# Attention keys stored in three orders, three contiguous products per dilated unit, and four gate projections at the first sweep's end

## The chip, the cores and the metric

The kernel runs on one core of a Trainium2 chip, as one program. The metric is the time of one execution in microseconds on the device, as a median of several runs. Beside it stands one execution taken by the hardware profiler, from which all views come. The engines are named as in the profile: PE multiplies matrices (PEld are its weight loads), DVE, ACT and POOL work on vectors, SP and ACT issue transfers (DMA).

## The reference

One decoder layer on 2048 tokens of width 1024: a combined projection to q, k, v (8 heads of 64) and the gated path's u and g (512 each); attention over three dilations; a gMLP gate; an output projection; an MLP of width 4096.

```python
WINDOW_DILATIONS = ((128, 1), (512, 4), (2048, 16))
...
h = rms_norm(x, norm1_g[l])
proj = jnp.einsum('bsd,de->bse', h, w_in[l])
q, k, v, u, g = jnp.split(...)
q = rms_norm(q.reshape(B, S, ATTN_HEADS, HEAD_DIM), q_norm_g[l])
k = rms_norm(k.reshape(B, S, ATTN_HEADS, HEAD_DIM), k_norm_g[l])
a = dilated_attention(q, k, v)
m = spatial_gating(jax.nn.gelu(u), jax.nn.gelu(g), ...)
mix = jnp.concatenate([rms_norm(a, attn_out_g[l]), rms_norm(m, gmlp_out_g[l])], axis=-1)
x = x + jnp.einsum('bse,ed->bsd', mix, w_out[l])
h = rms_norm(x, norm2_g[l])
f = jnp.square(jax.nn.relu(jnp.einsum('bsd,df->bsf', h, w_ff1[l])))
x = x + jnp.einsum('bsf,fd->bsd', f, w_ff2[l])
```

For each dilation d, position t attends to t, t-d, t-2d and so on, down to t-window (128 steps back). The three branches are combined by their softmax denominators, so they can share one maximum per position and head.

## The kernel before

Numbers are kept as pairs of a high part of reduced precision (F32R) and a low rest; a product of two such pairs is three PE products (hi x hi, lo x hi, hi x lo).

**Sweep 1** (0 to 387 us of the profile) runs over 16 tiles of 128 tokens. For each, `gemm3` projects q, k and v with 24 products of 512 columns each; a tile later `behind` transposes q and k, splits them into parts and stores them head by head in DRAM: `kt_d` holds a head's keys, 64 rows of high and 64 of low parts by 2048 tokens in their natural order, `qt_d` the queries with tokens sorted by their residue modulo 16, and `v_d` the values. Sorting happens in `store_q`, once for every group G of four tiles: a copy (ACT for high, POOL for low parts) into a tile `qp`, of which there are two, and two DMAs on SP, for each of the four pairs of heads `pr`. `max1`, `max4` and `fold4` work out score maxima of dilations 1 and 4, which go to `mx_d`.

**The transition** (387 to 421 us): the gate projections of the last two tiles, 14 and 15, then `rest` with maxima that DVE paces, and the loads and maxima (`group`, product `ps_mx`) of head 0.

**Attention** (421 to about 731 us) runs over 8 heads of 20 jobs each. Jobs 0 to 7 are dilation 1, two units each; then, for each residue r of 0 to 3, two jobs of dilation 4 (two units each) and one of dilation 16 (four units). A unit is a block of 128 keys against the queries that see them: keys are the product's weights, queries its moving operand. Each unit has two products: 128 rows of keys `ks` (high and low parts) against `qh`, the high part of the queries held twice; and 65 rows, 64 of high keys `k2` and one of ones, against `q2`, the low part of the queries and a row with minus the maximum. For dilations 4 and 16 the weights are read from `ks` and `k2` with a stride of 4 or 16 elements (lines 830 and 837). Then DVE adds the mask in PSUM, ACT writes the exponential twice (`ph`, rounded, and `e`), POOL makes the rest `pl` = e - ph, and the job's products with the values, `pv`, run four jobs later (PD = 4). In jobs 5, 8, 11 and 14 (MXAT) four `ps_mx` products each find the dilation-16 maxima of the next head, with the 64 rows of the high parts. The loads of the next head (`prepare`) stand at the start of the head before, V's behind jobs 4 and 12.

In all of this SP, PE, DVE and POOL work strictly in program order (`InOrder`), so that whatever a waiting instruction of a queue is followed by, waits with it. A DMA also waits for the one that last used its semaphore, eight of which go round over the queues of SP and ACT.

**Sweep 2** (731 to 1150 us) projects u and, for all tiles but 14 and 15, the gate (`gemm_g`, 24 products of 512 columns), then does the output projection. The **MLP** (to the end) is not touched.

Of the kernel before, what the change touches and what calls it, by code (L numbers as in the profile page):

```python
# [30 lines left out]
PD, PB, EB, LOL, EVL = 4, 5, 4, 2, 1  # L31
# [4 lines left out]
MXAT = (5, 8, 11, 14)  # L36
V1AT, V4AT = 12, 4
# [3 lines left out]
GEAT = 13  # L41
# [19 lines left out]
PSB, MXB, HS0 = 4, 1, 0  # L61

# [41 lines left out]
def tile_hybrid_block(  # L104
# [35 lines left out]
    qt_d = dram.tile([H, P, S], F32, name="qt_d")  # L140
    kt_d = dram.tile([H, P, S], F32, name="kt_d")
# [4 lines left out]
    ge_d = dram.tile([2, P, GW], F32, name="ge_d")  # L146
# [169 lines left out]

    mk1 = mkp_pool.tile([P, 2, 256], F32, name="mk1")
# [16 lines left out]
    m4t, m4e = masks(4)  # L334
    m16t, m16e = masks(16)
# [4 lines left out]
    def sweep1():  # L340
        if True:
# [8 lines left out]
            wh = [zh] + [[wp.tile([P, AW], F32R, name=f"wh{c}_{k}") for k in range(KD)] for c in (1, 2)]  # L350
            wl = [zl] + [[wp.tile([P, AW], F32R, name=f"wl{c}_{k}") for k in range(KD)] for c in (1, 2)]
# [68 lines left out]
            def store_q(G):  # L420

                for pr in range(NG):
                    for part, src in ((0, f32(qhis[G])), (1, qlos[G])):
                        src = src[:, pr, :].rearrange("p (i s) -> p s i", s=16)
                        end = G == NT // 4 - 1
                        tag = "qn" if part == 0 and end else "qp"
                        queue = nc.scalar if part == 1 and end else nc.sync
                        qp = sp.tile([P, AW], F32, tag=tag, name="qp", bufs=2).rearrange("p (s i) -> p s i", s=16)
                        if part == 0:
                            nc.scalar.activation(qp, src, AF.Copy)  # L430
                        else:
                            nc.gpsimd.tensor_copy(qp, src)  # L432
                        for hh in range(2):
                            queue.dma_start(
                                qt_d[2 * pr + hh, part * HD : (part + 1) * HD, :].rearrange("d (s i) -> d s i", s=16)[
                                    :, :, G * 32 : (G + 1) * 32
                                ],
                                qp[hh * HD : (hh + 1) * HD],
                            )
# [65 lines left out]
            qhis, qlos = {}, {}  # L505
# [41 lines left out]

            last = None
            gsrc = w_in[:, 3 * AW + GW : 3 * AW + 2 * GW]
            for t in range(NT):  # L550
# [5 lines left out]
                for c in range(3):  # L556
# [53 lines left out]
    def attention(finish, xnp, xs, tpe, wu):  # L610
        with ExitStack() as st:
# [12 lines left out]
            def prepare(h):  # L624
# [31 lines left out]
                def group(r0, psm=psm, queue=sy):  # L656
# [836 lines left out]
```

## Time and profile before

| what | value |
|---|---|
| median of 3 runs | 2432.99 us (2431.91 to 2437.35) |
| the profiled execution | 2441.18 us |
| its span | 2439.5 us |
| its mean granted PE clock | 0.963 |
| PE busy | 2357.1 us (97%) |
| PE clock in the transition, 386 to 421 us | 0.58 |
| PE clock in the attention, 421 to 731 us | 0.85 |
| PE clock in the MLP, 1150 to 2439 us | 0.99 |
| DMA busy share in the transition and the attention | 0.98 and 0.64 |

The three clocks are means of the windows between the stages' bounds. A window's row gives its length, then busy time and instruction count for each engine, then the granted clock, the share of time in which the 16 DMA engines were busy, and what they moved in GB/s. A timeline's row gives start, length, engine, line, operation, output and inputs, rows and columns; in brackets stands the time that the engine sat idle before it and what ended it. Matmuls overlap, so the pace is read from start to start, not from a length.

### The profile page before, as it was taken

What the parts mean: (1) busy time and instruction counts of PE and PEld (TensorE: products, weight loads), DVE (VectorE), ACT (ScalarE), POOL (GpSimd) and SP (SyncE); (2) the same over time, 40 slices, a digit from 0 to 9 for tenths busy, and PEclk for the clock granted to TensorE, in tenths of its full rate; (3) what the DMA queues carried; (4) which work ended last, traced back from release to release, by engine and by line L of the source; (5) the groups of instructions that cost most, each with busy time, mean ns of one, the idle gap of its engine ahead of it and who ended that gap; (6) DMA issues with size and microseconds to landing.
All of it is one profiled execution on the core that took longest, in us unless ns stands there. A gap on an engine that the chain in (4) does not pass through costs nothing. (4 is left out here: it accounts for less than half of the span.)

```text
span 2439.5 us, 31701 instructions
## 1 busy us (share of the span) xinstructions
PE 2357.1 (97%) x11292; PEld 1958.9 (80%) x11292; DVE 1461.1 (60%) x2940; ACT 973.0 (40%) x1584; POOL 843.3 (35%) x657
## 2 busy tenths in 40 slices
PE   8999997999997999998989999999999999999999
PEld 6777775999996788886778887788878888888887
DVE  6556666565565665665775557655557566565542
ACT  5323222656673222223544555555543232222321
POOL 1000001555551122222566666667752001131210
PEclk9999997789898999998999999999999999999999
DMA  6435247656744433333666556654559665575652
GB/s 195 87 79 118 61 101 166 187 150 192 197 148 104 102 89 97 92 89 117 203 191 191 150 154 194 195 155 148 155 177 335 217 198 190 182 241 180 190 172 78
DMA packets 432301, 382.34 MB, mean 157 GB/s; under 512 B 89704, under 2 KB 358632, under 8 KB 427528
## 3 DMA queue, kind: packets, MB, share of 16 engines
q1 hardware_dynamic: 415408, 377.68, 53.1%
q10 hardware_dynamic: 16736, 2.65, 0.7%
q8 instruction: 89, 1.46, 0.3%
q14 instruction: 68, 0.56, 0.1%
HBM read 259.80 MB, written 120.39 MB: 156 GB/s over the span
## 5 line engine op out<-in xcount | busy, mean ns | idle before, releaser
L1292 PE MATMUL ps_f<-hop,wop 128*128 128x512 f32 x2688 | 620.1, 392 | 11.9 <-ACT c L1300 3.2
L1414 PE MATMUL ps_f<-split 128*128 128x512 f32 x2688 | 611.1, 390 | 2.8 <-ACT c L1279 2.8
L1292 PEld LDWEIGHTS ps_f<-hop,wop 128*128 128x128 f32 x2688 | 507.6, 189 | 122.7 <-ACT hop L188 4.3
L1414 PEld LDWEIGHTS ps_f<-split 128*128 128x128 f32 x2688 | 505.8, 188 | 108.2 <-ACT c L1279 3.2
L1204 POOL TENSOR_TENSOR as<-w1r 128x512 f32<-128x512 f32 x160 | 213.5, 1342 | 164.9 <-DVE wop L189 149.6
L188 ACT ACTIVATE split<-sr 128x1024 fp32r<-128x1024 f32 x112 | 118.4, 1060 | 330.5 <-PE ps_f L1414 325.6
L1204 POOL TENSOR_TENSOR c<-c 128x512 f32<-128x512 f32 x160 | 233.7, 1485 | 45.0 <-ACT c L1280 30.7
L1424 DVE TENSOR_TENSOR acc<-acc,ps_f 128x512 f32<-128x512 f32 x192 | 124.4, 682 | 206.1 <-PE ps_f L1414 205.9
L1204 POOL TENSOR_TENSOR raw<-raw 128x1024 f32<-128x1024 f32 x40 | 101.4, 2543 | 420.8 <-DMA raw<-in_w_ff_dram 388.6
L74 POOL TENSOR_TENSOR pl<-e,ph 128x512 fp32r<-128x512 f32 x144 | 175.6, 1231 | 154.8 <-ACT e L74 127.0
L189 DVE TENSOR_TENSOR wop<-as,wop 128x512 fp32r<-128x512 f32 x160 | 149.5, 935 | 91.3 <-ACT wop L188 88.9
L188 ACT ACTIVATE wop<-as 128x512 fp32r<-128x512 f32 x160 | 100.3, 629 | 214.0 <-POOL as L1204 128.0
L74 DVE TENSOR_TENSOR ps_as<-ps_as,mk 128x512 f32<-128x512 f32 (+1 forms) x160 | 105.7, 663 | 122.8 <-PE ps_as L74 112.9
L189 DVE TENSOR_TENSOR split<-sr,split 128x1024 fp32r<-128x1024 f32 x112 | 162.9, 1455 | 16.6 <-ACT split L188 12.0
L74 PE MATMUL ps_o<-ph,v 128*64 128x128 f32 (+3 forms) x816 | 154.0, 276 | 1.4 <-ACT nacc L74 1.4
L74 PE MATMUL ps_as<-qh,ks 128*128 128x256 f32 (+1 forms) x384 | 143.0, 378 | 0.0
L74 ACT ACTIVATE ph<-ps_as 128x512 fp32r<-128x512 f32 (+1 forms) x160 | 92.4, 577 | 126.8 <-DVE ps_as L74 126.6
L432 POOL COPY qp<-qlo 128x512 f32<-128x512 f32 x16 | 17.1, 1074 | 363.5 <-DVE qlo L411 155.3
L74 PE MATMUL ps_as<-q,k 65*128 65x256 f32 (+1 forms) x384 | 139.1, 370 | 0.0
L452 DVE CUSTOM_DVE_ANT_0 jk<-ps_sc,mk 128x256 f32<-128x256 f32 (+1 forms) x232 | 92.5, 399 | 53.3 <-PE ps_sc L448 47.2
L74 PEld LDWEIGHTS ps_o<-ph,v 128*65 128x65 f32 (+1 forms) x816 | 114.4, 157 | 1.6 <-ACT nacc L74 1.6
L74 PEld LDWEIGHTS ps_as<-qh,ks 128*128 128x128 f32 x384 | 108.0, 281 | 3.0
(262 smaller groups left out, 4080.8 us busy)
## 6 DMA issues: line engine op xcount, KB each, us to landing
s_d<-c SPq DMA_DIRECT2D x224, 256.0 KB, 2.2
sr<-s_d SPq DMA_DIRECT2D x112, 512.0 KB, 3.6
raw<-in_w_ff_dram SPq DMA_DIRECT2D x96, 512.0 KB, 4.8
w1r<-in_w_ff_dram SPq DMA_DIRECT2D x128, 256.0 KB, 3.2
v<-v_d SPq DMA_DIRECT2D x24, 1040.0 KB, 12.8
xt<-in_x_dram SPq DMA_DIRECT2D x32, 512.0 KB, 4.1
raw<-h_d SPq DMA_DIRECT2D x28, 512.0 KB, 5.5
v_d<-vt SPq DMA_DIRECT2D x16, 520.0 KB, 6.2
```

What stands on the lines that cost most here:

```text
L74: return self.tc.keep_in_program_order(op(*args, **kwargs))
L188: en.scalar.activation(dst_hi, raw, AF.Copy)
L189: (en.gpsimd if on_pool else en.vector).tensor_tensor(dst_lo, raw, f32(dst_hi), ALU.subtract)
L432: nc.gpsimd.tensor_copy(qp, src)
L452: order[1].tensor_tensor_reduce(jk[:, :n], ps[:, j, :n], mk, 1.0, -3e38, ALU.add, ALU.max, accum_out=m[:, col : col + 1])
L1204: nc.gpsimd.tensor_tensor(dst, a, b, op)
L1292: nc.tensor.matmul(ps[bank], a[:, k, :], b[k], start=first and k == n == 0, stop=(k == 3 and n == 2), skip_group_check=True,)
L1414: nc.tensor.matmul(ps, s[a][:, k, :], t[b][:, k % 2, :], start=k == m == 0, stop=k == NH - 1 and m == 2)
L1424: nc.vector.tensor_tensor(c, c, ps, op)
```

## The change

1. Keys are stored three times: `kt_d` as before, `k4_d` with tokens sorted by residue modulo 4, `k16_d` modulo 16. `store_g` makes 24 sorted copies for each of the first three groups, nearly all on POOL, with 48 DMAs on SP (before, 8 copies and 16 DMAs); `qp` has three buffers. Of the last group only pair 0 is stored in sweep 1; the 18 copies and 36 DMAs of pairs 1 to 3 stand in `finish`, behind head 0's first loads.
2. Dilation 4 and 16 read their weights contiguously from tiles `k4` and `k16`. A unit there has three products: 128 rows against `qh`, 65 rows against `q2` (whose row 64 is zero), and 66 rows of a constant `sel` that picks out row 65 of `q2`, minus the maximum. `ps_mx` runs over 128 rows, with `qh` and `k16`. `k1` and `k4` have one buffer: `k4` of a head is loaded at the head's start, `k1` of the next behind job 9.
3. The value projections of tiles 14 and 15 move behind the last q and k, and the gate projections of tiles 12 and 13, with their x loaded and transposed again, join those of 14 and 15 there; sweep 2 has two gate projections fewer. The masks of dilations 4 and 16 are made at the transition.

```diff
@@ constants
-PD, PB, EB, LOL, EVL = 4, 5, 4, 2, 1
+PD, PB, EB, LOL, EVL = 4, 5, 3, 1, 1
...
-MXAT = (5, 8, 11, 14)
-V1AT, V4AT = 12, 4
+MXAT = (6, 9, 11, 13)
+V1AT, V4AT, K1AT = 12, 4, 9
...
-GEAT = 13
+PRE = (14, 15, 12, 13)
...
+QPB = 3
@@ DRAM
-    qt_d = dram.tile([H, P, S], F32, name="qt_d")
-    kt_d = dram.tile([H, P, S], F32, name="kt_d")
+    qt_d, kt_d, k4_d, k16_d = (dram.tile([H, P, S], F32, name=f"{n}_d") for n in ("qt", "kt", "k4", "k16"))
@@ sweep 1, the stores of a group of four tiles
-            def store_q(G):
-                for pr in range(NG):
-                    for part, src in ((0, f32(qhis[G])), (1, qlos[G])):
...
-                        qp = sp.tile([P, AW], F32, tag=tag, name="qp", bufs=2).rearrange("p (s i) -> p s i", s=16)
-                        if part == 0:
-                            nc.scalar.activation(qp, src, AF.Copy)
-                        else:
-                            nc.gpsimd.tensor_copy(qp, src)
...
+            def store_by(dst, m, G, pr, part, src, sync):
+                end = G == NT // 4 - 1
+                n = 512 // m
+                tag = "qn" if part == 0 and end else "qp"
+                qp = sp.tile([P, AW], F32, tag=tag, name="qp", bufs=2 if tag == "qn" else QPB).rearrange("p (s i) -> p s i", s=m)
+                src = f32(src).rearrange("p (i s) -> p s i", s=m)
+                if end and part == 0 and pr == 0:
+                    nc.scalar.activation(qp, src, AF.Copy)
+                else:
+                    nc.gpsimd.tensor_copy(qp, src)
+                if sync is None:
+                    sync = nc.scalar if part == 1 and end else nc.sync
+                for hh in range(2):
+                    rows = dst[2 * pr + hh, part * HD : (part + 1) * HD, :].rearrange("d (s i) -> d s i", s=m)
+                    sync.dma_start(rows[:, :, G * n : (G + 1) * n], qp[hh * HD : (hh + 1) * HD])
+
+            def store_g(G, todo, sync=None):
+                cols = slice((G % 2) * 512, (G % 2 + 1) * 512)
+                for pr, part in todo:
+                    k, q = (klos[G][:, pr, :], qlos[G][:, pr, :]) if part else (kring[:, pr, cols], qhis[G][:, pr, :])
+                    store_by(qt_d, 16, G, pr, part, q, sync)
+                    store_by(k16_d, 16, G, pr, part, k, sync)
+                    store_by(k4_d, 4, G, pr, part, k, sync)
...
                     if tg == 3:
-                        store_q(G)
+                        store_g(G, [(pr, part) for part in (1, 0) for pr in range(NG)] if G < NT // 4 - 1 else ((0, 0), (0, 1)))
@@ sweep 1, its end
                 for c in range(3):
+                    if c == 2 and t >= NT - 2:
+                        behind(t - 1, *last, c)
+                        continue
...
             for t in (NT - 2, NT - 1):
                 _, xh, xl, r = xs[t]
                 ps = psm.tile([P, AW], F32, tag="mm", name="ps_mm")
+                gemm3(ps, [(xh[:, k, :], xl[:, k, :], wh[2][k], wl[2][k]) for k in range(KD)])
+                keep_v(t, ps, r)
+            for n, t in enumerate(PRE):
+                if t < NT - 2:
+                    xs[t] = load_x_t(xp, pst, t, newton=True)
...
-            def finish(pe, dve):
+            def finish(pe, dve, sy):
                 order[:] = pe, dve
+                store_g(G, [(pr, part) for pr in range(1, NG) for part in (0, 1)], sy)
@@ attention, the loads of a head
-                sy.dma_start(f32(qh[0:HD, :]), qt_d[h, 0:HD, :])
-                sy.dma_start(f32(ks[0:HD, :]), kt_d[h, 0:HD, :])
-                sy.dma_start(f32(ks[HD:P, :]), kt_d[h, HD:P, :])
+                sy.dma_start(f32(k16), k16_d[h])
+                for half in range(2):
+                    sy.dma_start(f32(qh[half * HD : (half + 1) * HD, :]), qt_d[h, 0:HD, :])
                 sy.dma_start(f32(q2[0:HD, :]), qt_d[h, HD:P, :])
-                sy.dma_start(f32(qh[HD:P, :]), qt_d[h, 0:HD, :])
-                sy.dma_start(f32(k2[0:HD, :]), kt_d[h, 0:HD, :])
...
+                def load_k(m):
+                    k = first.pop(m, None)
+                    if k is None:
+                        k = (tp if m == 1 else sp).tile([P, S], F32R, tag=f"k{m}", name=f"k{m}", bufs=1)
+                    T.append(k)
+                    sy.dma_start(f32(k), (kt_d if m == 1 else k4_d)[h])
+                    if m == 1:
+                        sy.dma_start(f32(k2[0:HD, :]), kt_d[h, 0:HD, :])
@@ attention, the products
-                        pe.matmul(ps[:, j, :], qh[0:HD, s * P : (s + 1) * P], ks[0:HD, s::16], start=True, stop=True)
+                        pe.matmul(ps[:, j, :], qh[:, s * P : (s + 1) * P], k16[:, s * P : (s + 1) * P], start=True, stop=True)
...
-                for ks, k2, qh, q2, w in units:
-                    pe.matmul(ps[:, n : n + w], ks, qh, start=True, stop=False)
-                    pe.matmul(ps[:, n : n + w], k2, q2, start=False, stop=True)
+                for pairs, w in units:
+                    for j, (k, q) in enumerate(pairs):
+                        pe.matmul(ps[:, n : n + w], k, q, start=j == 0, stop=j == len(pairs) - 1)
...
+                def three(k, q, q2):
+                    return (k, q), (k[0 : HD + 1], q2[0 : HD + 1]), (sel[0 : HD + 2], q2)
...
-                            kk, qq = slice(s0, s0 + 509, 4), slice(32 * cb, 32 * cb + n)
-                            units.append((ks[:, kk], k2[:, kk], qv[:, r, :, qq], q2v[:, r, :, qq], 4 * n))
+                            kk, qq = slice(512 * r + cb * P, 512 * r + (cb + 1) * P), slice(32 * cb, 32 * cb + n)
+                            units.append((three(k4[:, kk], qv[:, r, :, qq], q2v[:, r, :, qq]), 4 * n))
...
-                        kk, qq = slice(s, None, 16), slice(s * P, (s + 1) * P)
-                        units.append((ks[:, kk], k2[:, kk], qh[:, qq], q2[:, qq], P))
+                        kk = slice(s * P, (s + 1) * P)
+                        units.append((three(k16[:, kk], qh[:, kk], q2[:, kk]), P))
@@ attention, the loop over heads
             for h in range(H):
+                load_k(4)
                 jobs = head_jobs(h, T)
...
+                    if h + 1 < H and i == K1AT:
+                        load_k(1)
@@ sweep 2
-                if t >= NT - 2:
+                if t in PRE:
                     return None
```

On PE, in head 0, a group of maxima products for head 1 and a job of dilation 4 with a whole and a half unit, before (`ks` and `k` are the two key tiles, `qh` and `q` the queries, `ps_o` the first value product behind):

```order
L74 MATMUL ps_mx<-ks,qh 128x128 x4
L74 MATMUL ps_as<-qh,ks 128x256
L74 MATMUL ps_as<-q_3869,k_3870 128x256
L74 MATMUL ps_as<-qh,ks 128x128
L74 MATMUL ps_as<-q_3869,k_3870 128x128
L74 MATMUL ps_o<-ph,v_4137 65x4x64
```

The same place on PE in the changed kernel, where k_4401 is head 1's `k16` and k_4398 head 0's `k4`:

```order
L75 MATMUL ps_mx<-k_4401,qh 128x128 x4
L75 MATMUL ps_as<-qh,k_4398 128x256
L75 MATMUL ps_as<-q_4142,k_4398 128x256
L75 MATMUL ps_as<-q_4142,sel 128x256
L75 MATMUL ps_as<-qh,k_4398 128x128
L75 MATMUL ps_as<-q_4142,k_4398 128x128
L75 MATMUL ps_as<-q_4142,sel 128x128
L75 MATMUL ps_o<-ph,v_4479 65x4x64
```

Two products of a unit have become three. On SP, from head 0's first loads to those of head 1, before (k_3870 is `k2`, v_3881 is V of dilation 1):

```order
L74 DMA k_3870<-kt_d 64x2048
L74 DMA v_3881<-v_d 128x16x130
L74 DMA qh<-qt_d 64x2048
L74 DMA ks<-kt_d 64x2048 x2
L74 DMA q_4058<-qt_d 64x2048
L74 DMA qh<-qt_d 64x2048
```

And in the changed kernel, with what each waits for, the start of the stores that now stand between them (k_d with runs of 32 is `k16_d`, with runs of 128 `k4_d`):

```order
L75 DMA v_4108<-v_d 128x16x130 [waits DMAHW7_49,PE_49]
L75 DMA qt_d<-qp 1024x1x32 [waits DMAHW0_49,Pool_49]
L75 DMA qt_d<-qp 1024x1x32 [waits DMAHW1_49]
L75 DMA k_d<-qp 1024x1x32 [waits DMAHW2_49,Pool_49]
L75 DMA k_d<-qp 1024x1x32 [waits DMAHW4_49]
L75 DMA k_d<-qp 256x1x128 [waits DMAHW5_49,Pool_49]
L75 DMA k_d<-qp 256x1x128 [waits DMAHW6_49]
L75 DMA qt_d<-qp 1024x1x32 [waits DMAHW7_49]
L75 DMA qt_d<-qp 1024x1x32 [waits DMAHW0_49]
L75 DMA k_d<-qp 1024x1x32 [waits DMAHW1_49]
L75 DMA k_d<-qp 1024x1x32 [waits DMAHW2_49]
L75 DMA k_d<-qp 256x1x128 [waits DMAHW3_49]
```

The last row shown is the eleventh of the 36 stores; the semaphore DMAHW3 that it waits for was last used by ACT's store of the maxima behind `rest(range(4, 8))`. The load of `k4` for head 0 and the loads of head 1 follow the 36th. On POOL, the last rows ahead of head 0's first `pl` in the changed kernel:

```order
L429 COPY qp<-kring 128x512
L429 COPY qp<-qhi 128x512
L429 COPY qp<-kring 128x512
L429 COPY qp<-qlo 128x512
L429 COPY qp<-klo 128x512 x2
L429 COPY qp<-kring 128x512
L659 MEMSET q_4403 2x2048
L75 TENSOR_TENSOR pl<-e,ph 128x512 x7
```

Before, only two small copies and a memset stood there; now the copies of the moved stores do, each of which needs a `qp` buffer that an earlier store has left. On PE, the end of the first sweep in the changed kernel (the last gate projection's last products, then `rest`, `ps_mx` and head 0):

```order
L226 MATMUL ps_mm<-zl_3618,xh 128x512
L227 MATMUL ps_mm<-zh_3614,xl 128x512
L479 MATMUL ps_tr<-ident,m_4023 8x128
L501 MATMUL ps_tr<-ident,m_4055 8x128 x4
L75 MATMUL ps_sc<-kring,qhi 128x256 x8
L75 MATMUL ps_tr<-ident,m_4055 8x128 x4
L75 MATMUL ps_mx<-k_4140,qh 128x128 x16
L75 MATMUL ps_mx<-ident,m_4150 16x128
L75 MATMUL ps_sc<-kring,qhi 128x256 x16
L75 MATMUL ps_tr<-ident,m_4055 8x128 x4
L75 MATMUL ps_as<-qh,k_4107 128x256
```

The maxima's `ps_sc` products of the last tile that stood behind the gates now stand ahead of them, and four gate projections instead of two precede `rest`.

More of the change, by code (lines that the diff above doesn't have):

```diff
@@ L349, in sweep1 @@
             zh, zl = wg_tiles()
-            wh = [zh] + [[wp.tile([P, AW], F32R, name=f"wh{c}_{k}") for k in range(KD)] for c in (1, 2)]
-            wl = [zl] + [[wp.tile([P, AW], F32R, name=f"wl{c}_{k}") for k in range(KD)] for c in (1, 2)]
+            wh, wl = {0: zh}, {0: zl}
+            for w, c in ((wh, 2), (wh, 1), (wl, 1), (wl, 2)):
+                w[c] = [wp.tile([P, AW], F32R, name=f"w{'h' if w is wh else 'l'}{c}_{k}") for k in range(KD)]
             vts = []
@@ L514, in behind @@
                         qhis[G] = sp.tile([P, NG, 512], F32R, tag="qhi", name="qhi")
-                        qlos[G] = sp.tile([P, NG, 512], F32, tag="qlo", name="qlo", bufs=1)
-                    los["k"] = sp.tile([P, NG, P], F32R, tag="klo", name="klo")
+                        qlos[G] = sp.tile([P, NG, 512], F32R, tag="qlo", name="qlo", bufs=1)
+                        klos[G] = sp.tile([P, NG, 512], F32R, tag="klo", name="klo", bufs=1)
                     pos = t % 8
@@ L546, in late4, with keep_v @@
                     store_m(G, range(H))
+            def keep_v(t, ps, r):
+                vt = vts[t % 2]
+                split_sb(vt[:, :, 0:HD], vt[:, :, HD + 2 : VW], ps.rearrange("p (h d) -> p h d", d=HD), r)
+                nc.sync.dma_start(v_d[:, t * P : (t + 1) * P, :].rearrange("h t c -> t h c"), f32(vt))
             last = None
@@ L641, in prepare @@
                 V = {}
-                T = [ks, qh, k2, q2, V]
+                T = [qh, q2, k16, V]
+                def load_k(m):
[6 more added lines that the diff above has]
+                        sy.dma_start(f32(k2[0:HD, :]), kt_d[h, 0:HD, :])
                 def load_v(part):
                     if part == 1:
-                        V[1] = v_tile(tp, "v1")
+                        V[1] = first.pop("v", None)
+                        if V[1] is None:
+                            V[1] = v_tile(tp, "v1")
                         sy.dma_start(f32(V[1]), v_d[h].rearrange("(b i) c -> i b c", i=P))
@@ L664, in row @@
                         dve.tensor_scalar(nm, ps[:16, 0, :], -1.0, None, ALU.mult)
-                        queue.dma_start(f32(q2[HD : HD + 1, :]), f32(nm))
+                        queue.dma_start(f32(q2[HD + 1 : HD + 2, :]), f32(nm))
                     def turn():
@@ L681, in group @@
                     return reduce
-                return T, group, load_v
+                return T, group, load_v, load_k
             later, splits = [], []
@@ L692, in due @@
                     f()
-            T, group, load_v = prepare(0)
+            T, group, load_v, load_k = prepare(0)
+            load_k(1)
             load_v(1)
             act.activation(root, ones_c, AF.Exp)
-            more = finish(pe, dve)
+            more = finish(pe, dve, sy)
             if X0S is None:
@@ L754, in head_jobs @@
             def head_jobs(h, T):
-                ks, qh, k2, q2, V = T
+                qh, q2, k16, V, ks, k4 = T
                 nacc = sp.tile([HD + 1, S], F32, tag="nacc", name="nacc")
@@ L896, in attention @@
                 if h + 1 < H:
-                    T, group, load_v = prepare(h + 1)
+                    T, group, load_v, load_k = prepare(h + 1)
                 for i, (units, msk, fin) in enumerate(jobs):
```

85 lines of the change are left out of this document (38 added, 47 removed).

## The prediction

> **What bounds the kernel now.** I read the chain of work that ended last, then the table of windows head by head, then timelines of single products. The chain is TensorE (PE) almost alone, and the page's largest lines on it belong to the MLP, which the change doesn't touch. What can be won has to come from the attention, cut here at the starts of its eight heads.
>
> ```profile
> PE 35%; DMA 1%; POOL 1%; issue 1%; ACT 0%; DVE 0%; SPq 0%; DVEq 0%; POOLq 0%; ACTq 0%
> core 0: us, PE busy (x) PEld busy (x) DVE busy (x) ACT busy (x) POOL busy (x), PEclk, DMA share, GB/s
> 421.00:461.00 40.00, 39.99 (x235) 38.86 (x236) 20.02 (x58) 22.69 (x43) 21.61 (x18) 0.69 0.56 145
> 461.00:505.00 44.00, 44.00 (x292) 43.08 (x291) 24.08 (x64) 25.92 (x48) 22.70 (x19) 0.73 0.68 178
> 505.00:540.00 35.00, 35.00 (x258) 34.19 (x257) 21.33 (x60) 22.92 (x42) 20.93 (x18) 0.95 0.66 177
> 540.00:574.00 34.00, 34.00 (x253) 33.19 (x252) 21.14 (x59) 22.55 (x43) 21.77 (x18) 1.00 0.74 199
> 574.00:611.00 37.00, 37.00 (x269) 36.19 (x268) 21.96 (x62) 23.61 (x44) 21.77 (x18) 0.91 0.71 188
> 611.00:655.00 44.00, 44.00 (x292) 43.08 (x292) 24.10 (x64) 25.98 (x48) 22.52 (x19) 0.73 0.68 177
> 655.00:690.00 35.00, 35.00 (x259) 34.19 (x258) 21.34 (x60) 22.76 (x42) 21.08 (x18) 0.95 0.79 233
> 690.00:727.00 37.00, 34.63 (x258) 33.98 (x256) 26.02 (x36) 28.80 (x55) 23.17 (x18) 0.91 0.33 118
> sum 306.00, PE 303.63 PEld 296.74 DVE 179.97 ACT 195.23 POOL 175.56; mean PE 37.95 PEld 37.09 DVE 22.50 ACT 24.40 POOL 21.94
> ```
>
> PE has no idle time in heads 0 to 6, and PEld, the weight loads, is nearly as full; no other engine is near its limit. The same program takes 34 us where the granted clock is 1.00 and 44 where it is 0.73. So two things are lost: clock, and time in which a product waits for its weights.
>
> ```profile
> 471.00:485.00 14.00, 14.00 (x81) 13.49 (x80) 6.53 (x24) 8.64 (x16) 7.31 (x7) 0.83 1.02 307
> 485.00:502.00 17.00, 17.00 (x94) 16.77 (x94) 7.14 (x19) 8.08 (x15) 7.10 (x6) 0.50 0.15 35
> 502.00:521.00 19.00, 19.00 (x151) 18.46 (x149) 12.00 (x31) 13.04 (x25) 11.38 (x10) 0.95 1.02 261
> ```
>
> Inside a head the clock falls in the part with strided keys (here 0.50) and comes back with the next head's dilation-1 jobs.
>
> **Term 1, the weights.** Start to start at full clock, in head 3:
>
> ```profile
> 542.19 0.29 PE L74 MATMUL ps_as<-q,k 65*128 65x256 f32 x1
> 542.32 0.29 PE L74 MATMUL ps_as<-qh,ks 128*128 128x256 f32 x1
> 542.44 0.29 PE L74 MATMUL ps_as<-q,k 65*128 65x256 f32 x1
> 542.56 0.23 PE L74 MATMUL ps_o<-ph,v 128*65 128x128 f32 x1
> ...
> 553.05 0.39 PE L74 MATMUL ps_as<-qh,ks 128*128 128x128 f32 x1
> 553.27 0.38 PE L74 MATMUL ps_as<-q,k 65*128 65x128 f32 x1
> 553.49 0.39 PE L74 MATMUL ps_as<-qh,ks 128*128 128x128 f32 x1
> ...
> 555.51 0.40 PE L74 MATMUL ps_as<-qh,ks 128*128 128x256 f32 x1
> 555.75 0.40 PE L74 MATMUL ps_as<-q,k 65*128 65x256 f32 x1
> 555.98 0.40 PE L74 MATMUL ps_as<-qh,ks 128*128 128x256 f32 x1
> 556.22 0.39 PE L74 MATMUL ps_as<-q,k 65*128 65x256 f32 x1
> 556.45 0.28 PE L74 MATMUL ps_o<-ph,v 128*65 128x256 f32 x1
> ...
> 557.08 0.69 PE L74 MATMUL ps_mx<-ks,qh 64*128 64x128 f32 x4
> 557.70 0.51 PE L74 MATMUL ps_as<-qh,ks 128*128 128x256 f32 x1
> ```
>
> With contiguous keys a 256-column product takes (542.56 - 542.19)/3 = 0.122 us, with keys at stride 4 (556.45 - 555.51)/4 = 0.235, with keys at stride 16 and 128 columns 0.22; an mx product takes 0.62/4 = 0.155. For 128 columns on contiguous weights the nearest row is the transposes of the second sweep, 8 in 0.79 us, 0.10 each:
>
> ```profile
> 1096.94 1.03 PE L276 MATMUL ps_tr<-ident,xt 128*128 128x128 f32 x8
> 1097.73 0.48 PE L225 MATMUL ps_mm<-woh,mh 128*128 128x512 f32 x1
> ```
>
> I take 0.11, between 0.10 and 0.122. The change gives each such unit a third product, so a full dilation-4 unit goes from 2 x 0.235 = 0.47 to 3 x 0.122 = 0.366 (12 per head: 1.25 us), the four half ones and the 16 of dilation 16 from 0.44 to 0.33 (20 x 0.11 = 2.2), the 16 mx products from 0.155 to 0.11 (0.7). Together 4.2 us a head, **33 us** in eight; the dilation-1 jobs stay. A head at full clock would be 34.0 - 4.2 = 29.8 us.
>
> ```profile
> L74 PEld LDWEIGHTS ps_as<-qh,ks x384: 186/312/339, 421.1 to 725.0; 128*128 128x128 f32 x192
> ```
>
> The loads' minimum of 186 ns is that of contiguous keys, the median of 312 that of strided ones. [...]
>
> The change also lets mx run on 128 rows instead of 64. I give that no price of its own: here no row has both counts with the same stride. [...]
>
> **Term 2, the clock.** The eight windows hold 306 us, 8 x 34 = 272, and head 7 has 2.4 us of idle PE: 306 - 272 - 2.4 = **32 us** go to the clock. In the strided part a 256-column product streams 0.12 us of its 0.235, in the new form all of its 0.122, so the array is fuller just where the clock falls. I take all 32, with 0 as the other bound, since in head 3 the same program kept its clock and the old part is thus near the edge. [...]
>
> **Term 3, the transfers.** Per head the loads of keys and queries grow from 3.15 to 5.24 MB (three key tensors of 1.05, the low half's 0.52, qh twice 0.52, q2 0.52). In head 3 DMA was busy 0.74 x 34 = 25.2 us with 199 GB/s, 6.8 MB. The 2.1 MB more take 6.8 us at 307 GB/s and 8.0 at 261, both rows above with a full DMA. So 32 to 33.2 us of transfers stand against 29.8 of PE: DMA becomes the bound of heads 1 to 6. Also k4 has one buffer and can be fetched only after the old head's last dilation-4 job; behind it k16 and qh of the next head must land before job 6, some 7 us into the head, where mx reads them: 3.1 MB need 10 to 12 us. I take 32.5 a head: 6 x 2.7 = **16 us** are given back. Bounds: 30 (nothing) and 36.
>
> **Term 4, head 0.** The order shows the last group's stores for pairs 1 to 3 (18 copies on POOL, 36 DMAs) between V1's load and k4's on SP, and on POOL ahead of the first pl. One of the stores (k4_d, the eleventh) waits, on a shared DMA semaphore, for the maxima's store behind rest(4..8), which is the last thing before head 0; 26 are left then.
>
> ```profile
> 103.38 23.27 SPq L434 DMA_DIRECT2D qt_d<-qp  x16
> ...
> L432 POOL COPY qp<-qlo 128x512 f32<-128x512 f32 x16 | 17.1, 1074 | 363.5 <-DVE qlo L411 155.3
> ...
> L74 POOL TENSOR_TENSOR pl<-e,ph 128x512 fp32r<-128x512 f32 x144 | 175.6, 1231 | 154.8 <-ACT e L74 127.0
> ```
>
> Sixteen such stores took 23.3 us with two buffers, 1.45 each; at that pace 26 need 38 us. Now five buffers serve them, two for the high and three for the low parts, and by bytes alone 3.4 MB at 261 GB/s would be 13. I take 24, between the two. The last copy stands some 6 us ahead of the last store, and the first pl behind it. PE runs ahead only by five jobs of scores, 20 products or 2.4 us, and then waits for pl: about 17 us. Then k4 (1 MB), k16 and qh of head 1 follow on SP, 9 us or more after the stores, while mx of head 1 stands at job 6: another 11. I take **28 us**, bounds 10 and 40.
>
> **Term 5, the end of sweep 1.**
>
> ```profile
> 385.95 0.39 PE L225 MATMUL ps_mm<-zh,xh 128*128 128x512 f32 x1
> 386.17 0.39 PE L226 MATMUL ps_mm<-zl,xh 128*128 128x512 f32 x1
> 386.40 0.39 PE L227 MATMUL ps_mm<-zh,xl 128*128 128x512 f32 x1
> ...
> 404.35 3.64 PE L74 MATMUL ps_mx<-ks,qh 64*128 64x128 f32 x16 [2.75 <-DMA ks<-kt_d]
> ```
>
> Two gate gemms of 24 products at 0.226 us, 10.9 us, leave sweep 2, where PE has no gaps, and come in here with 16 more transposes (1.6 us) and two waits for x's split. What they can hide is DVE's pace in rest() and the 2.75 us wait for keys, yet DVE's maxima are queued behind the same PE order. I take **+1 us** net (-6 to +6). The reordered value products cost nothing: only their place changes.
>
> **Term 6, sweep 1.** Each of the first three groups has 24 copies on POOL (26 us at 1.07) and 48 DMAs on SP instead of 16. x is loaded some tiles ahead, so SP's burst of about 45 us hides there; but the next tile's qlo and klo have one buffer and wait for the low copies, 12 pairs in about 23 us against a tile of 23.3. I take **+3 us** (0 to 12).
>
> **The sum.** -33 - 32 + 16 + 28 + 1 + 3 = -17 us, against the profiled execution's 2441.2 us (span 2439.5 and 1.7 outside it): 2424, or 0.9930 of it. The median of the runs is 2433.0, 0.3% under the profiled one; the same share of it gives **2416 us**.
>
> **The rivals**, at the median's level.
> - *Nothing collides*: the stores run at the rate of their bytes, k16 lands in time, DMA hides. Head 0 loses 10 instead of 28, heads 1 to 6 take 30: 2416 - 18 - 15 = 2383. For it: DMA stands at 0.74 in head 3 and much faster loads occur (307 GB/s). Against: the order on SP and POOL. 0.20.
> - *The clock stays as it is*: term 2 is lost, but a head is then 29.8 + 4 = 33.8 us by PE, which hides the 32.5 of the transfers, and term 3 goes with it: 2416 + 32 - 16 = 2432. For it: stalls on DMA thin out the array again. Against: the denser strided part, and head 3. 0.14.
> - *Slower, the transfers set every head*: at 235 GB/s, between the 199 of head 3's mean and the 261 above, a head's 8.9 MB take 38 us instead of 32.5, and the late mx stalls PE so that the clock falls too: 6 x 5.5 + 8 = 41, 2457. It decides from 35.4 us a head on, 17/6 = 2.9 over the value taken, where the sum is 0. 0.18.
> - *It doesn't do what it says*: strided weights gone but the loads' time not, since weight loads from contiguous 65 and 66 rows are no shorter. Terms 1 and 2 fall, and 256 products more at 0.235 us add 60: 2541. The 186 ns of the dilation-1 keys speak against it. 0.02.
>
> **How the numbers follow.** The forecast has 0.46. A measurement of this kernel tells about 0.2%, 5 us, from no change. Faster than 2428: the forecast mostly (0.40), the first rival (0.20) and some of the second (0.05): 0.65. Within: 0.15. Slower: 0.20. The range reaches from the first rival, a little further down for bounds of terms 5 and 6, to the middle between the second and third: 2375 to 2445.
>
> **What would show it.** In the new profile: weight loads of ps_as in strided jobs near 187 ns (term 1); granted clock of 0.95 or more in heads 2 to 6 (term 2); heads 1 to 6 at 30 to 36 us with PE idle before ps_mx or behind k4, k16, qh (term 3); in head 0 an idle PE of some 17 us before the first ps_o, released by POOL, with qp copies just ahead on POOL (term 4); head 0's first product at 430 to 435 us instead of 421 and sweep 2 shorter by 11 (term 5). Wrong it would be, above all, if SP's queue does not stand still at the eleventh store, or if the heads go at PE's 29.8 us.

## The result, and the profile after

The changed kernel takes 2518.61 us, median of four runs (2510.84 to 2528.23), beside 2432.45 us of the kernel before (2427.13 to 2437.35). The ratio is 1.0357, with the interval 1.0312 to 1.0401: **slower**, where 2416 us was forecast, and above the whole range. The profiled execution took 2528.23 us (span 2526.5, mean clock 0.955), 87.0 us more span than before. A ratio below leaves out executions more than 1.5% above the fastest of their kernel; there are two of them, both of sort_sb64. Cut at the ends of the stages, in us, with the forecast's terms put into the same stages:

| stage, up to | before: ends, takes | after: ends, takes | difference | forecast |
|---|---|---|---|---|
| sweep 1 and transition: first `ps_as` | 421.1, 421.1 | 471.1, 471.1 | +50.0 | +14.9 (terms 5 and 6, and the two gates) |
| attention: last `nacc` | 731.0, 309.9 | 813.0, 341.9 | +32.0 | -21 (terms 1 to 4) |
| sweep 2: first `ps_f` | 1179.6, 448.6 | 1267.5, 454.5 | +5.9 | -10.9 (the two gates) |
| MLP: end of the span | 2439.5, 1259.9 | 2526.5, 1259.0 | -0.9 | 0 |
| sum | | | +87.0 | -17 |

The chain of waits still reads as one engine. That it says PE is what hides the loss: it follows what released what, and a product on a halved clock is PE too.

```profile
PE 34%; DMA 1%; DVE 1%; POOL 1%; issue 1%; ACT 0%; SPq 0%; POOLq 0%; DVEq 0%
```

First the weights, of the tile `ps_as` (duration in ns as minimum, median and maximum, then first and last start):

```profile
L75 PEld LDWEIGHTS ps_as<-qh,k x384: 186/190/336, 471.1 to 806.6; 128*128 128x128 f32 x192
```

The median load fell from 312 to 190 ns, as term 1 said. The windows of the whole attention, of before and then of after, show PE's busy time:

```profile
421.00:731.00 310.00, 307.15 (x2127) 299.88 (x2128) 182.87 (x459) 199.11 (x368) 177.47 (x147) 0.85 0.64 176
```
```profile
471.00:813.00 342.00, 276.31 (x2383) 271.33 (x2384) 176.68 (x461) 198.42 (x368) 192.13 (x161) 0.86 0.77 219
```

PE is busy 276.3 us instead of 307.2, 30.8 less, with 256 products more. But it now stands idle 342.0 - 276.3 = 65.7 us, where it was 2.9, and the clock stayed at 0.86 (0.85): half clock covers 95.9 us of it, where it covered 93.2. PE's waits in that stretch (sum, times, longest) name the idle time:

```profile
PE ps_mx L75 <- DMA qh<-qt_d: 35.6, 7, 9.9
PE ps_o L75 <- POOL pl L75: 22.5, 3, 21.4
PE ps_mx L75 <- DVE m L75: 4.7, 14, 0.5
```

So 58 of the 66 us are two things: `ps_mx` waits for `qh`, once in each of heads 0 to 6, and head 0 waits for its first `pl`. The windows of heads 1 to 6 show the first:

```profile
530.00:571.00 41.00, 34.78 (x304) 34.26 (x303) 21.74 (x66) 24.13 (x46) 22.06 (x19) 0.88 0.73 220
571.00:609.00 38.00, 33.84 (x300) 33.33 (x298) 21.28 (x61) 23.61 (x45) 21.61 (x19) 0.91 0.85 236
609.00:647.00 38.00, 34.44 (x302) 33.75 (x300) 21.92 (x67) 24.34 (x46) 22.12 (x19) 0.91 0.82 241
647.00:685.00 38.00, 33.53 (x298) 33.01 (x298) 21.17 (x59) 23.52 (x45) 21.62 (x18) 0.91 0.80 237
685.00:725.00 40.00, 33.49 (x296) 33.12 (x297) 20.85 (x57) 23.21 (x44) 21.19 (x19) 0.87 0.82 226
725.00:765.00 40.00, 34.77 (x312) 34.11 (x310) 22.64 (x70) 25.14 (x49) 22.97 (x20) 0.91 0.83 226
```

A head takes 38 to 41 us, 38.8 by the spacing of its maxima's step `nm` on DVE (38.1 before), not 32.5. DMA is at 0.73 to 0.85 and not full, so its mass doesn't set the pace. In the third of these heads the timeline has

```profile
628.53 1.12 PE L75 MATMUL ps_mx<-k,qh 128*128 128x128 f32 x4 [2.62 <-DMA qh<-qt_d]
```

and the windows around it

```profile
620.00:624.00 4.00, 4.00 (x42) 4.00 (x41) 3.40 (x5) 3.67 (x8) 3.58 (x3) 1.00 1.04 297
624.00:628.00 4.00, 1.91 (x19) 1.65 (x17) 2.30 (x3) 2.94 (x6) 4.00 (x5) 1.00 1.02 223
628.00:632.00 4.00, 3.47 (x19) 3.47 (x20) 1.40 (x9) 0.80 (x3) 1.15 (x1) 0.55 0.99 257
632.00:636.00 4.00, 4.00 (x26) 4.00 (x26) 1.09 (x2) 2.10 (x4) 1.82 (x2) 0.60 1.04 431
636.00:640.00 4.00, 3.98 (x38) 3.84 (x36) 2.06 (x10) 2.88 (x5) 0.47 (x1) 1.00 1.07 363
```

The wait ends, and then the clock is halved for 6.8 us: 19 to 26 products in a window instead of 42. Over heads 1 to 6 the waits are 25.7 us and the halved stretches behind them 47.8, of which half, 24, is lost; (25.7 + 24)/6 = 8.3 us a head, and 38.8 - 8.3 = 30.5 is what is left.

Head 0 and the stages before it, from PE's timeline:

```profile
408.72 0.79 PE L225 MATMUL ps_mm<-zh,xh 128*128 128x512 f32 x1 [7.32 <-ACT zh L191]
...
428.06 0.79 PE L225 MATMUL ps_mm<-zh,xh 128*128 128x512 f32 x1 [5.71 <-ACT xh L195]
...
442.84 0.80 PE L225 MATMUL ps_mm<-zh,xh 128*128 128x512 f32 x1 [5.44 <-ACT xh L195]
...
496.95 0.48 PE L75 MATMUL ps_o<-pl,v 128*65 128x256 f32 x1 [21.45 <-POOL pl L75]
...
512.43 1.12 PE L75 MATMUL ps_mx<-k,qh 128*128 128x128 f32 x4 [9.95 <-DMA qh<-qt_d]
```

The late gates wait three times, 18.5 us together, and run their first products 0.43 us apart instead of 0.23. POOL's and SP's timelines at head 0's stall:

```profile
492.62 1.07 POOL L429 COPY qp<-kring 128x512 f32<-128x512 f32 x1 [0.59 <-DMA qt_d<-qp]
493.75 1.80 POOL L659 MEMSET q<- 2x2048 f32 x1
```
```profile
464.90 0.38 SPq L75 DMA_DIRECT2D v<-v_d  x1
465.37 3.27 SPq L75 DMA_DIRECT2D qt_d<-qp  x2
...
496.37 2.83 SPq L75 DMA_DIRECT2D k_d<-qp  x4
499.31 1.05 SPq L75 DMA_DIRECT2D k<-k_d  x2
```

All 36 stores stand from 465.37 to 499.2, 0.94 us each; the first `pl` comes behind the last copy and a memset, and k4 and `qh` for the next `ps_mx` behind the last store.

### The profile page after: what moved, and what is told of

Read it like the earlier page. It is cut to its first block, busy times and chain, and to the rows that moved or that the text cites. A ratio compares the mean times of both kernels' runs of the same rounds, so it can differ in the third digit from the quotient of the medians.

```text
span 2526.5 us, 32588 instructions
## 1 busy us (share of the span) xinstructions
PE 2352.1 (93%) x11564; PEld 1946.0 (77%) x11564; DVE 1471.4 (58%) x2954; ACT 966.7 (38%) x1583; POOL 926.7 (37%) x736
## 5 line engine op out<-in xcount | busy, mean ns | idle before, releaser
L1245 POOL TENSOR_TENSOR c<-c 128x512 f32<-128x512 f32 x160 | 233.9, 1487 | 44.6 <-ACT c L1321 30.4
L189 DVE TENSOR_TENSOR split<-sr,split 128x1024 fp32r<-128x1024 f32 x112 | 156.6, 1399 | 18.1 <-ACT split L188 13.3
L75 DVE TENSOR_TENSOR ps_as<-ps_as,mks 128x512 f32<-128x512 f32 (+1 forms) x128 | 83.2, 653 | 114.2 <-PE ps_as L75 70.2
L75 PE MATMUL ps_o<-ph,v 128*64 128x128 f32 (+3 forms) x816 | 144.6, 264 | 1.9 <-ACT nacc L75 1.9
L75 PE MATMUL ps_o<-pl,v 128*65 128x128 f32 (+1 forms) x408 | 102.8, 263 | 23.5 <-POOL pl L75 22.5
L225 PE MATMUL ps_mm<-zh,xh 128*128 128x512 f32 x232 | 97.9, 423 | 19.9 <-ACT xh L195 12.6
L75 PE MATMUL ps_as<-qh,k 128*128 128x256 f32 (+1 forms) x384 | 114.9, 304 | 0.0
L75 PE MATMUL ps_as<-q,k 65*128 65x128 f32 (+3 forms) x384 | 112.5, 300 | 0.0
```

The lines of the kernel that those rows point to most:

```text
L75: return self.tc.keep_in_program_order(op(*args, **kwargs))
L189: (en.gpsimd if on_pool else en.vector).tensor_tensor(dst_lo, raw, f32(dst_hi), ALU.subtract)
L225: en.tensor.matmul(ps, ah, bh, start=(i == 0), stop=False)
L1245: nc.gpsimd.tensor_tensor(dst, a, b, op)
```

## The experiments

Times are medians, each ratio is to the kernel before on the same chip in the same minutes (2433.3 to 2436.7 us), with its 95% interval. "Attention" is the time from the first `ps_as` to the last `nacc` in the profiled execution.

### The waits in the heads

**mx_late**: the changed kernel, the next head's maxima later.

```diff
-MXAT = (6, 9, 11, 13)
+MXAT = (8, 10, 12, 14)
```

> The changed kernel with the four groups of ps_mx behind jobs 8, 10, 12 and 14 instead of 6, 9, 11 and 13. Theory W, in heads 1 to 6 PE waits at the first group for k16 and qh of the next head (2.6 us in head 2) and then runs 4 to 7 us at half clock: without that wait the heads fall from 38.5 to 34 us or less, the time by 20 to 35 us to about 2490. Rival B, the transfers' mass sets the head: PE waits elsewhere instead (k4, V, the next head's k1), heads stay at 37 to 39 us and the time within 8 us of 2518.

2500.07 us, 1.0271 (1.0229 to 1.0313); attention 312.5 instead of 341.9. Four windows of 40 us in heads 2 to 5, then two of PE's waits:

```profile
551.00:591.00 40.00, 39.19 (x382) 38.82 (x380) 28.61 (x70) 32.05 (x61) 30.61 (x26) 1.00 0.98 275
591.00:631.00 40.00, 38.23 (x365) 37.73 (x365) 26.04 (x81) 28.23 (x54) 25.02 (x21) 1.00 1.02 298
631.00:671.00 40.00, 39.26 (x382) 38.88 (x381) 27.14 (x83) 29.71 (x56) 27.54 (x23) 1.00 1.03 280
671.00:711.00 40.00, 39.45 (x386) 38.86 (x385) 27.89 (x71) 29.57 (x56) 26.87 (x23) 1.00 0.97 283
```
```profile
PE ps_o L75 <- POOL pl L75: 19.5, 1, 19.5
...
PE ps_mx L75 <- DMA qh<-qt_d: 8.9, 4, 7.1
```

With the wait gone the clock stays at 1.00 and a head takes 32.0 us, close to the 32.5 of the forecast. The place of the four groups, not the mass of the transfers, which is unchanged, made 38.8 of it. That the transfers now set the pace is not shown: DMA is full, but PE is busy 156.1 of these 160 us, 31.2 a head, and waits for transfers some 0.5 us a head.

**mx_late64**: the same with the maxima over 64 rows, as before the change.

```diff
-pe.matmul(ps[:, j, :], qh[:, s * P : (s + 1) * P], k16[:, s * P : (s + 1) * P], start=True, stop=True)
+pe.matmul(ps[:, j, :], qh[0:HD, s * P : (s + 1) * P], k16[0:HD, s * P : (s + 1) * P], start=True, stop=True)
```

> mx_late (the changed kernel, groups behind jobs 8, 10, 12 and 14) with ps_mx on 64 rows, contiguous. In mx_late heads 2 to 5 ran 160 us at a clock of 1.00. Theory R: falls at half clock come back in the dilated jobs of heads 2 to 6, 10 to 30 us in all, the time 2510 or more. Theory D: with contiguous keys and three products the array is dense enough, clock 1.00 and 2500 within 8 us.

2491.66 us, 1.0230 (1.0201 to 1.0258); clock 1.00 for 198 us on end, and 0.962 as the mean of the profiled execution, beside 0.959 in mx_late. The 64 rows of `ps_mx` did not pull the clock down here, as theory D had it.

**m128, m128_late, mx8_before**: in the kernel before, `ps_mx` on 128 rows; that with the later places; the later places alone.

```diff
-pe.matmul(ps[:, j, :], qh[0:HD, s * P : (s + 1) * P], ks[0:HD, s::16], start=True, stop=True)
+pe.matmul(ps[:, j, :], qh[:, s * P : (s + 1) * P], ks[:, s::16], start=True, stop=True)
-MXAT = (5, 8, 11, 14)
+MXAT = (8, 10, 12, 14)
```

> The kernel before with one line changed: its maxima products ps_mx run over 128 rows (high and low parts of the keys, still at stride 16) instead of 64. Theory R, the clock falls because products on 64 rows count for less in what the clock follows: granted clock of the attention up from 0.85 to 0.95 or more, heads near 34 us, the time 20 to 32 us below before (2400 to 2413). Theory D, the clock follows only how densely columns stream: 64 or 128 rows make no difference, heads stay at 34 to 44 us and the time within 6 us of before (2427 to 2439).

> The kernel before with ps_mx over 128 rows and its groups behind jobs 8, 10, 12 and 14 instead of 5, 8, 11 and 14, so that the second half of qh has landed. Theory R, 64-row products let the clock fall: the waits of m128 on qh (38 us in all) are gone, no fall of 10 to 20 us at half clock is left in heads 1 to 6, heads near 34 us, the time 20 to 30 us below before (2407 to 2417). Theory D, only the density of the columns counts: the falls of before return, the time within 6 us of before.

> The control for m128_late: the kernel before with the groups behind jobs 8, 10, 12 and 14, on 64 rows as before. Theory R: falls at half clock as before, some 30 us lost, the time within 8 us of before. Theory P, that the place of the groups and not their rows keeps the clock: as fast as m128_late.

2474.98 us, 1.0160 (1.0125 to 1.0196); 2465.18, 1.0115 (1.0088 to 1.0141); 2454.11, 1.0073 (1.0047 to 1.0099). What was expected of m128 failed: PE's waits in it show a cause that no theory had,

```profile
PE ps_mx L74 <- DMA qh<-qt_d: 38.3, 5, 9.3
```

for the kernel before loads the second half of `qh` behind the keys and `q2`, and 128 rows need it (in m128_late the same wait is still 24.9 us). So neither m128 kernel tells anything of rows. mx8_before, expected within 8 us of before, is 18 us slower: half clock covers 105 us of its attention instead of 93. Why the old places keep more of the clock was not settled.

**q64 and q128** take that wait away: in the kernel before the second half of `qh` is loaded at once behind the first, and the groups stand at jobs 10, 12, 13 and 14; q128 has m128's edit as well.

```diff
-MXAT = (5, 8, 11, 14)
+MXAT = (10, 12, 13, 14)
 sy.dma_start(f32(qh[0:HD, :]), qt_d[h, 0:HD, :])
+sy.dma_start(f32(qh[HD:P, :]), qt_d[h, 0:HD, :])
...
-sy.dma_start(f32(qh[HD:P, :]), qt_d[h, 0:HD, :])
```

> The kernel before with the second half of qh loaded right behind the first and the groups of ps_mx behind jobs 10, 12, 13 and 14, still on 64 rows. Control for q128. Theories D and R alike: falls at half clock in the strided jobs as before, 20 to 35 us lost in all; the time 2435 to 2460.

> q64 with ps_mx on 128 rows. Theory R, 64-row products bring the clock down: no falls of 10 us or more in heads 1 to 6, attention at 280 to 290 us, 20 to 30 us faster than q64. Theory D, spacing alone counts: the same falls and the same time as q64 within 8 us.

2472.69 us, 1.0145 (1.0125 to 1.0166), and 2471.04, 1.0142 (1.0117 to 1.0166): alike, but both above the 2435 to 2460 expected, as these places cost still more clock (157 us at half clock in q64's attention, 138 in q128's). A window of q64, then of q128:

```profile
460.00:500.00 40.00, 37.41 (x250) 35.91 (x250) 19.43 (x55) 22.18 (x42) 20.66 (x17) 0.76 0.66 173
```
```profile
460.00:500.00 40.00, 37.14 (x255) 36.65 (x253) 20.55 (x58) 22.80 (x44) 20.42 (x18) 0.80 0.65 173
```

Rows made no difference to the time in the kernel with strided weights either. Running `ps_mx` over 128 rows, a part of the change, brings nothing that these runs can see.

### The stores

**late_undone**: the changed kernel without its third part (values and gates of the last tiles where they were).

```diff
-PRE = (14, 15, 12, 13)
+PRE = (14, 15)
...
-                    if c == 2 and t >= NT - 2:
-                        behind(t - 1, *last, c)
-                        continue
...
-            for t in (NT - 2, NT - 1):
...
-                keep_v(t, ps, r)
```

> The changed kernel with its third part undone: value products of tiles 14 and 15 in their old place, gates of tiles 12 and 13 again in sweep 2. Theory Q, the late products cost by their waits at the first sweep's end (7.3, 5.7 and 5.4 us of idle PE ahead of them, each followed by some 4 us at half clock) and their 11 us come out nowhere in sweep 2: head 0's first product moves from 471 to about 435 us, sweep 2 stays at 450 us, the time falls by 30 to 40 us to 2480 to 2490. Rival S, the waits are those of the stores and of rest() and only move to other instructions: the first product comes 11 us earlier, sweep 2 grows by 11, and the time stays within 10 us of 2518.

2523.66 us, 1.0362 (1.0318 to 1.0406), as slow as the change. The first `ps_as` comes 10.6 us earlier (460.5) and sweep 2 takes 448.9 us again, but the attention takes 352.0, 10 more. PE's waits, from the transition on:

```profile
PE ps_mx L75 <- DMA qh<-qt_d: 51.1, 8, 15.3
PE ps_o L75 <- POOL pl L75: 21.2, 3, 20.2
```

The longest wait for `qh` is that of head 0's maxima in the transition. The late products had covered it.

**stores_back**: the changed kernel with all stores of the last group in sweep 1.

```diff
-... if G < NT // 4 - 1 else ((0, 0), (0, 1)))
+... if G < NT // 4 - 1 else [(pr, part) for pr in range(NG) for part in (0, 1)])
...
-                store_g(G, [(pr, part) for pr in range(1, NG) for part in (0, 1)], sy)
```

> The changed kernel with all four pairs' sorted stores of the last group in the first sweep, none behind head 0's loads. Theory Q, the 31 us of idle PE in head 0 (21.4 before the first value product, 10.0 before ps_mx) are those of the moved stores: they vanish, head 0's first product comes some 10 us later because its loads stand behind the stores, and the time falls by 15 to 25 us to about 2498. Rival S, the same 24 us of stores delay head 0's loads by as much as they delayed its first value product: the time stays within 6 us of 2518.

2525.60 us, 1.0366 (1.0329 to 1.0403). Head 0's stall is gone (attention 311.6), but another stands ahead of the gates, from 422 to 456 us, and the first `ps_as` comes at 496.9. Among PE's waits is

```profile
PE ps_mm L225 <- ACT xh L195: 37.9, 2, 34.1
```

as ACT, which splits x for the gates, has DMAs of the stores ahead of that in its queue.

**late_stores_mx**: stores_back, late_undone and mx_late in one.

> The changed kernel with late groups (as mx_late), without the late value and gate products (as late_undone) and with all stores in sweep 1 (as stores_back). Each was tried alone: -18, +5 and +7 us. Theory C, they hide each other, since the stores' 24 us delay whatever stands behind them until nothing waits: head 0 without a stall (-31), sweep 2 at 449 us (-4), the first product near 465 us: the time 2455 to 2470. Rival, the stores hold up ACT's queue as in stores_back (34 us ahead of the gates): first product at 490 us, the time 2480 to 2500.

2481.38 us, 1.0186 (1.0157 to 1.0216); attention only 279.5, but the first `ps_as` at 489.2, behind

```profile
PE ps_mx L75 <- DMA qh<-qt_d: 45.2, 7, 37.8
```

Here head 0's maxima wait for the whole of the stores. The attention behind them gains 30.4 us over the kernel before, of the 49 that terms 1 to 3 promised together.

**twice_tail**: mx_late with the 36 late stores made twice (the second time the same data).

```diff
                 store_g(G, [(pr, part) for pr in range(1, NG) for part in (0, 1)], sy)
+                store_g(G, [(pr, part) for pr in range(1, NG) for part in (0, 1)], sy)
```

> mx_late with the last group's 36 sorted stores of pairs 1 to 3 made twice. Theory Q, these stores stand on the path of head 0: at 0.9 to 1.4 us each the second set adds 30 to 50 us, all of it as idle PE in head 0 ahead of the first value product (19.5 us in mx_late), and the time is 2530 to 2550. Rival, head 0 waits for something else (the maxima's store, the loads' own rate): less than 10 us more, 2500 to 2510.

2538.93 us, 1.0425 (1.0385 to 1.0465), 39 us above mx_late. The wait for `pl` grows from 19.5 us to

```profile
PE ps_o L75 <- POOL pl L75: 52.0, 3, 51.0
```

31.5 us for 36 more stores, 0.88 each. So the chain of copies and stores sets the stall, and nothing hides what is added to it.

### Sorted keys without the stores

**sort_sb**: sweep 1, the transition and sweep 2 as before; the attention of the change, but `k4` and `k16` are sorted in SBUF, out of the natural keys `k1`, by four copies each on DVE (on POOL for head 0's `k16`). Dilation 1 has three products as well.

```diff
-MXAT = (5, 8, 11, 14)
+MXAT = (8, 10, 12, 14)
+K4AT, K16AT = (0, 1, 2, 3), (4, 5, 6, 7)
...
+                def turn_k(eng, dst, m, j):
+                    w = m // 4
+                    d = dst.rearrange("p (s i) -> p s i", s=m)[:, j * w : (j + 1) * w]
+                    eng.tensor_copy(d, k1.rearrange("p (i s) -> p s i", s=m)[:, j * w : (j + 1) * w])
...
+                    if i in K4AT:
+                        turn_now(dve, k4, 4, K4AT.index(i))
+                    if h + 1 < H and i in K16AT:
+                        turn_k(dve, T[2], 16, K16AT.index(i))
```

> The first sweep, its end and sweep 2 as in the kernel before; the attention of the changed kernel, but k4 and k16 are made in SBUF from the natural keys by DVE (POOL for head 0), eight copies of 512 columns a head in jobs 0 to 7, instead of being stored and loaded in three orders. k2 is dropped, dilation 1 too has three products (16 more a head, 1.9 us at 0.122). Groups of ps_mx behind jobs 8, 10, 12, 14. Theory Q, the loss of the change lies in the sorted stores and not in the products: first product near 423 us, heads 31 to 34 us at a clock of 1.00, attention near 260 us instead of 310, the time 2380 to 2400. Rival V, DVE, busy 20 of 34 us a head and nearly full in dilation 1, takes the copies' 4 us badly: heads at 36 us or more, the time 2420 or more.

2421.03 us, median of ten runs, 0.9948 (0.9923 to 0.9973): it beats both kernels, by 0.5% over the one before, but by much less than theory Q expected; the time is that of rival V. First `ps_as` at 423.7, attention 287.7 instead of 309.9, half clock in 20 us of it, 10 of them right at its start. Two windows of a head each, and the copies:

```profile
495.00:530.00 35.00, 33.52 (x321) 33.15 (x320) 29.10 (x70) 24.03 (x46) 22.70 (x18) 1.00 0.64 188
530.00:565.00 35.00, 34.22 (x325) 33.60 (x323) 28.67 (x71) 24.47 (x46) 24.56 (x19) 1.00 0.64 187
```
```profile
L75 DVE CAST k<-k x60: 580/1130/1708, 426.0 to 677.2; 128x512 fp32r<-128x512 f32 x60
```

A head is 35 us at full clock, with 1.5 us of idle PE: the copies, 1.13 us each (the 4 us for eight in rival V were an estimate that no run shows), push DVE from 21 to 29 us a head, and short waits come with it. They are not all of what lies between 35 us and the 31.7 that 29.8 and 1.9 for the added products would give: PE itself is busy 33.5.

**sort_sb2** (the copies of `k16` in jobs 7 to 10, the groups in 11 to 14) and **sort_sb64** (`ps_mx` on 64 rows, the edit of mx_late64):

```diff
-MXAT = (8, 10, 12, 14)
-K4AT, K16AT = (0, 1, 2, 3), (4, 5, 6, 7)
+MXAT = (11, 12, 13, 14)
+K4AT, K16AT = (0, 1, 2, 3), (7, 8, 9, 10)
```

> sort_sb with the copies of k16 in jobs 7 to 10 and the groups of ps_mx behind jobs 11 to 14, that is outside of the dilation-1 jobs. Rival V: 5 to 15 us faster than sort_sb. Theory Q: within 6 us of it, or slower if the next head waits for its maximum's row.

> sort_sb with ps_mx on the 64 rows of the high parts, which need the first half of qh alone. Theory D, the clock goes by how densely the columns stream and not by rows: the clock stays at 1.00 in heads 1 to 6, the 7.3 us wait for qh ahead of head 0's ps_mx shrinks, and the time is 0 to 10 us below sort_sb (2411 to 2421), below both kernels of the case. Theory R, rows count: falls at half clock of 7 to 20 us a head come back in the dilated jobs, 2440 or more.

sort_sb2: 2488.42 us, 1.0231 (1.0201 to 1.0261), attention 352.6; PE waits 18.9 us for DVE's maxima, and 17 to 24 us of every head are at half clock. sort_sb64: 2431.27 us, the median of all twelve runs, and 0.9962 (0.9941 to 0.9984), with executions from 2414.61 us at a mean clock of 0.982 to 2460.25 at 0.959; its profiled one (2447.62) has two falls of 27.3 us each. Whether its rows or chance made these was not settled.

## Why the prediction was wrong

The span grew by 87 us where the forecast had it shrink by 17. Of these 104 us, 53 are in the attention, 35 ahead of it and 17 in sweep 2 (the MLP gave 1 back).

*Term 1, the weights, -33*: right in kind, and too large. Loads take 190 ns, and PE is busy 30.8 us less, though part of that is half clock that fell on idle time in head 0. At full clock PE is busy 31.2 us a head in mx_late, not 29.8, against 34.0 before: 2.8 a head instead of 4.2, an estimated 22 us in eight heads.

*Term 2, the clock, -32*: the step that failed first. The argument was that denser products keep the clock. They did where the heads had little to wait for (mx_late: 1.00 through heads 2 to 5; sort_sb: half clock in 20 us of 288). But the prediction itself put a stall into each head, and in its sum gave the stall no effect on the clock. Half clock went from 93.2 to 95.9 us, and heads 1 to 6 stood at 0.87 to 0.91 instead of 0.95 or more: the term brought nothing.

*Term 3, the transfers, +16*: the mechanism and the place were named, "k16 and qh of the next head must land before job 6, ... 3.1 MB need 10 to 12 us" against 7, which is 3 to 5 us, and 25.7/6 = 4.3 were measured. The price was taken from the mass instead, 32.5 a head, which could hold only if no product needs a tensor before it is there. The wait and the 4 us lost behind it came to 38.8. That mx_late's 32.0 lies near the 32.5 is in part luck, as PE's own work there, 31.2, is more than the 29.8 assumed. Terms 1 to 3 together are 49 us of the error: the attention without head 0's stall was forecast 49 us shorter and came out level (32.0 - 31.4).

*Term 4, head 0, +28*: right, 21.4 + 10.0 = 31.4. The pace taken for the stores was right (24 us for 26 is 0.92; 0.94 measured). One step was not: SP stood not at the eleventh store but already ahead of the first, so 36 were left, and PE waited 21 instead of 17.

*Terms 5 and 6, +1 and +3*: mis-sized, by 35 us up to the first `ps_as`. PE's busy time up to there grew by 30 us (windows: 401 to 432), of which 12.5 are the gates and transposes moved in, the rest slower products, as half clock there grew from 29.7 to 64.6 us; its idle time grew by 20. I had named "two waits for x's split" without a price: they took 11.1 us, the wait for the gate's weights `zh` 7.3, and each was followed by half clock, 4.6 to 5.8 us of it.

The claim that the stores hide in sweep 1 failed too. Up to the sweep's last `fold4`, before and then after, the products `ps_mm` alone give

```profile
0.00:377.74 377.74, 299.60 (x1167) 213.09 (x1167) 33.95 (x48) 33.04 (x48) 1.00 0.45 105
```
```profile
0.00:387.42 387.42, 301.68 (x1134) 209.97 (x1134) 32.36 (x46) 31.52 (x46) 0.98 0.54 121
```

It comes 9.7 us later with 33 products fewer ahead of it, 7.5 us at 0.227: some 17 us are lost in the sweep, where 3 (0 to 12) were forecast. In sort_sb, without the added stores, the same place comes at 378.3, behind 1167 products as before.

Part 3 is not the cause of the rest: late_undone, without it, is as slow. late_undone and sort_sb both lack it, and differ up to the first `ps_as` in the stores and in head 0's loads: 460.5 against 423.7 (421.1 before). What part 3 would do without the stores was not run.

*Sweep 2, -10.9*: +5.9. PE's busy time fell by 4.4 only (414.1 to 409.7), as half clock grew from 37.5 to 47.8 us, and its waits for x grew; PE's waits there, of before and of after:

```profile
PE ps_tr L266 <- DMA xt<-in_x_dram: 7.3, 7, 3.6
```
```profile
PE ps_tr L266 <- DMA xt<-in_x_dram: 16.3, 9, 5.2
```

The gates of tiles 12 and 13 were what PE did while the next x came: with them back, in late_undone, this wait is 8.8 us.

*The rivals.* The slower one had the outcome and half of the cause, "the late mx stalls PE so that the clock falls too", and its head of 38 us is what came; but it blamed the mass of the transfers, which mx_late refutes, and it kept term 5 at +1. The rival by which the clock stays as it is had that outcome (0.86 after 0.85) and its reason, "stalls on DMA thin out the array again"; but it let PE's time hide the transfers, so that these stalls cost nothing in its 2432.

## What to carry to other kernels

When a product is moved or widened, ask of each of its operands, half by half, when it lands; moving the four groups of maxima by one or two jobs was worth 0.9% here. Price a stall together with the clock behind it: some 4 us of waiting cost 8 here. And a data order that costs many small stores is better made where time is free (here in SBUF, on DVE: 2421 us) than at a stage's boundary, where the next stage's first loads stand behind the stores (2519).

## What the runs showed of the hardware

The granted clock takes two values in the traces of the kernel before and of the changed one, 0.5 and 1.0. Half clock comes in 23 stretches in the first and 30 in the second, of 3.41 us or a multiple of it, up to 34.13 and 23.89 us, but for the last of each, 2.10 and 2.33 us at the end of the span. A wait of 2.62 us was followed by 6.8 us at half clock (628.4 to 635.2), though of the two windows of 4 us ahead of it, both at 1.00, PE is busy 4.00 and 1.91. How much idle time it takes was not shown. Three stretches of 20.5 us in the kernel before, from 435.8, 483.6 and 633.7, have no idle PE in the 6.8 us ahead of them or in themselves.

A store of 128 KB took SP 0.94 us in a row of 36 with five buffers (the changed kernel, from 465.37), and 1.45 in a row of 16 with two (the kernel before, 23.27 us from 103.38). A kernel took the same time with its `ps_mx` products on 64 and on 128 rows (q64 and q128: 2472.69 and 2471.04 us).
